# One table re-layout on another DMA queue, small loads later, denser table building in a two-block transformer

## The chip, the core and the metric

The kernel runs on one core of a Trainium2 chip. The metric is the device time of one execution in microseconds (us): the median of three runs of the kernel before is 1490.93 us (1490.72 to 1493.30). About 0.2 % of it, 3 us, is what a measurement of this kernel can tell from no change.

## What is computed

One sequence of 256 tokens of width 1024 passes through two transformer blocks of two layers each, all in float32. The first block has a pooling and recurrent mixer, a banded attention, a cross attention to a memory and two MLPs. The change touches the end of the first block and most of the second:

```python
def second_block(x, ...):
    h = x
    for i in range(DEPTH):                       # DEPTH = 2
        u = rms_norm(h, norm_mix[i])
        if i % 2 == 0:
            mix = diff_attention(u, attn_w_qkv, q_gain, k_gain, lam_vecs, subln_gain, w_o, lam, cos, sin)
        else:
            mix = s5_layer(u, a_re, a_im, log_dt, b_re, b_im, c_re, c_im, d_skip, w_glu)
        h = h + mix
        h = h + square(relu(rms_norm(h, norm_ffn[i]) @ w_up)) @ w_down      # 1024 -> 4096 -> 1024
```

`diff_attention` makes q, k and v with one 1024x3072 weight, normalises and rotates q and k (cos, sin, two gains), and subtracts lam times a second softmax from the first. `s5_layer` is a two-way complex state-space scan over 64 groups of 16 channels, then `gelu`, then a 1024x2048 gated product (`w_glu`). The scan is computed in blocks of eight tokens: from the parameters alone the kernel first builds tables (called e, g, and t) that turn the scan inside a block into matrix products.

## The kernel before

Every large product is done on TensorE (PE) as three single-pass products of split operands, hi x hi, lo x hi and hi x lo. So each weight tile takes three steps ahead of its products: a DMA on the queue of SyncE (SP) into a `raw` tile (L42), a rounding copy `whi` on ScalarE (ACT, L47 or, with a gain, L53), and the rest `wlo` on VectorE (DVE, L49 or L58). There are four `raw` buffers and ten `whi`/`wlo` pairs. A DMA into `raw` is issued when the `wlo` that last read that buffer is done.

A scheduler decides the order of the instructions of each engine when the kernel is built; on the chip each engine then runs its list in that order and waits at the head of it. The same holds for SP's list of DMA issues and for those of GpSimd (POOL). Each DMA of SP has one of eight completion semaphores in turn, and an issue also waits for the DMA that had this semaphore before.

The tables of the scan don't depend on the tokens, so they are built beside two MLPs: `ssm_tables` is a generator, and `mlp` advances it by `rate` per step (`step`, 49 of them in an MLP; what is left runs at `step(1000)` near its end). Blocks 0 to 7 are built in the last MLP of the first block (632 to 847 us of the span) and blocks 8 to 15 in the first MLP of the second block (980 to 1183 us, called ffb0). Each block writes e (`d_e`), g (`d_g`) and a kernel of lags (`d_kl`) to device memory. At the end of each half two DMAs re-layout `d_kl` into `d_ks`, and eight DMAs `d_ks` into `d_tt`, the table t (L1450 to L1456), all of them issued by POOL.

Between the two MLPs comes the differential attention (`diff`, 847 to 980 us). Its weights follow those of the MLP on SP. `rotations` combines cos, sin and the gains (L661 to L674); `part` makes the products with the weights, k first; `prep` normalises and rotates, and its `turned` transposes the result `z` on PE (tile `tq`, L742). In front of `part` stand the residual `X` (L187 to L200) of the last MLP, for token tiles t0 and t1, and its transposes `tp` (L140) into `hh` and `hl`.

After ffb0 comes the scan stage (`ssm`, 1183 to 1288 us). It copies X into `xp` (L1522), transposes it (`utp`), and for each quarter b: products with e (`zt`, L1561), transposes `z`, a rotation on DVE (`ra`, `zb`), the scan (`so`, L1589), a reversal on ACT (`sr`), two products with phases on DVE (`h0`, `h1`, L1610 and L1611), the products with t and g (`yp`), and gelu; then `ytp`, and the products `val` and `gp` with `w_glu`. `ssm_prefetch` loads some tables ahead, and `ssm` puts two tables of g and two of e (e4, e5) into `raw` buffers, behind the first four tiles of `w_glu` that use the same four buffers.

Of the kernel before, what the change touches and what calls it, by code (L numbers as in the profile page):

```python
# [413 lines left out]
class Attn:  # L414
# [224 lines left out]
    def diff(self, pool, w_qkv, gain, q_gain, k_gain, lam_vecs, subln, w_o, cos2, sin2, done):  # L639

        nc = self.nc
        cs = pool.tile([128, 2, 64], F32, tag="cos", name="cos")
        sn = pool.tile([128, 2, 64], F32, tag="sin", name="sin")
        nc.sync.dma_start(out=cs, in_=cos2.rearrange("(t p) e -> p t e", p=128))
        nc.sync.dma_start(out=sn, in_=sin2.rearrange("(t p) e -> p t e", p=128))
        gq, gk = (pool.tile([128, 64], F32, tag="g" + nm, name="qkg") for nm in "qk")
        nc.sync.dma_start(out=gq, in_=q_gain.partition_broadcast(128))
        nc.sync.dma_start(out=gk, in_=k_gain.partition_broadcast(128))
        sg = pool.tile([128, KT], F32, tag="sg", name="sg")
        nc.sync.dma_start(out=sg, in_=subln)  # L650
        lv = pool.tile([128, 4, 64], F32, tag="lv", name="lv")
        nc.sync.dma_start(out=lv, in_=lam_vecs.partition_broadcast(128))
        nlam = pool.tile([128, 1], F32, tag="nlam", name="nlam")
        tabs = {}

        def rotations():
            for nm, g in (("k", gk), ("q", gq)):
                ta = pool.tile([128, 2, 64], F32, tag="ta" + nm, name="ta")
# [485 lines left out]
class Ssm:  # L1144
# [225 lines left out]
    def ssm_tables(self, blocks, bc4, gain, d_rows, dmask):  # L1370
# [6 lines left out]
        with self.tc.tile_pool(name="tab", bufs=1, reuse_waits="tile") as pool:  # L1377
# [73 lines left out]
            nc.gpsimd.dma_start(out=ks[a0:a1, :, :, 0:112], in_=kl5[a0:a1, :, 1, :, 32:144])  # L1451
            yield
            n = 4 * (a1 - a0)
            for r in range(8):
                src = bass.AP(self.d_ks.tensor, self.d_ks.offset + 4 * a0 * 16 * 240 + r * 16, [[240, 16], [3840, n], [1, 128]])
                nc.gpsimd.dma_start(out=self.d_tt[r * 16:r * 16 + 16, 4 * a0:4 * a1, :], in_=src)  # L1456
            yield

    def ssm_prefetch(self):

        self.pre_pool = self.tc.tile_pool(name="pre", bufs=1, side="right", reuse_waits="tile")
        self.pre = pool = self.pre_pool.__enter__()
        self.tbs = {}
        self.unit = {}
        self.rho = pool.tile([128, NG], F32, name="rho")
        self.nc.sync.dma_start(out=self.rho, in_=self.d_rho)
        for b in range(2):
            self.load_phases(b)
        for q in range(4):
            t = pool.tile([128, 1024], F32, name=f"e{q}")  # L1470
            self.load_units(t, "e", q)
        for q in range(2):
            self.load_units(pool.tile([128, 1024], F32, tag=f"w{q}", name=f"t{q}"), "t", q)
# [17 lines left out]
    def load_phases(self, b):  # L1491

        t = self.pre.tile([128, 3, 16, 32], F32, tag="tbs", name="tbs", bufs=2)
        self.nc.sync.dma_start(out=t, in_=self.d_c[b].rearrange("p (a g c) -> p a g c", a=3, g=16))
        self.tbs[b] = t
# [241 lines left out]
def first_block(c, A):  # L1737
    tc, nc = c.tc, c.nc
    for l in range(2):
# [38 lines left out]
        with tc.tile_pool(name=f"ff{l}", bufs=1, reuse_waits="tile") as pool:  # L1778
            if l == 1:
                c.later.append(lambda: reorder(c))  # L1780
            c.mlp(pool, A["w_ff1"][l], gc[2], A["w_ff2"][l], lambda t, a, q: c.residual(t, a, post, q), perm=l == 1,
                  fill=tables(c, A, range(8)) if l == 1 else c.ssm_scalars(A["ssm_a_re_2"], A["ssm_a_im_2"], A["ssm_log_dt_2"], c.sgn),
                  rate=0.7 if l == 1 else 0.2)

# [14 lines left out]
def tables(c, A, blocks, last=False):  # L1799
    yield from c.ssm_tables(blocks, A["ssm_bc"], A["ssm_g"], c.d_rows, c.dmask)  # L1800
    if last:
        c.ssm_prefetch()


def second_block(c, A, out):
# [5 lines left out]
    with tc.tile_pool(name="ffb0", bufs=1, reuse_waits="tile") as pool:  # L1811
        c.mlp(pool, A["ffn_w_up_2"][0], c.gcols[:, 8, :], A["ffn_w_down_2"][0], lambda t, a, q: c.residual(t, a, None, q, feat=False),
              fill=tables(c, A, range(8, 16), last=True), rate=0.85)
    with tc.tile_pool(name="ssm", bufs=1, reuse_waits="tile") as pool:
# [84 lines left out]
```

## Time and profile before

| what | value |
|---|---|
| median of the runs | 1490.93 us |
| the profiled execution | 1488.93 us |
| its span | 1487.2 us |
| PE busy | 1414.7 us, 95 % |
| DVE busy | 1103.8 us, 74 % |
| ACT busy | 859.4 us, 58 % |
| POOL busy | 234.4 us, 16 % |
| mean granted TensorE clock | 0.985 |

The span is the time from the first to the last instruction in the profiled execution; that execution took 1.73 us more than its span, and 2.0 us less than the median. PE's share is that of an engine that has its next product ready nearly always, so a change shows in PE's gaps: they add up to 72.5 us. A row of the waits names the instruction that waited, what it waited for, the microseconds in total, how often, and the longest. Stage limits are read from the timeline; all times of the trace count from the start of the span.

### The profile page before, as it was taken

To read this page: it belongs to the slowest core of one execution; us is meant where nothing else is said; L and a number is where in the kernel's file an instruction comes from. 1 tells how busy PE (TensorE), PEld (TensorE's weight loads), DVE (VectorE), ACT (ScalarE), POOL (GpSimd) and SP (SyncE) were. 2 spreads that over 40 slices of the span, in tenths; PEclk is the share of its full clock that TensorE was granted. 3 is DMA by queue.
4 is the path that set the end of the run, shared out by engine and by line. 5 is a ranking of instruction groups with operands and counts; after the bars stand their busy time and mean duration, and the time that the engine had idled before them with its cause. 6 is when DMAs were issued, how large, how long until landed. Compare 5 with 4: busy or idle time off the path is not lost.

```text
span 1487.2 us, 25549 instructions
## 1 busy us (share of the span) xinstructions
PE 1414.7 (95%) x9668; PEld 1231.5 (83%) x9668; DVE 1103.8 (74%) x1965; ACT 859.4 (58%) x1480; POOL 234.4 (16%) x290
## 2 busy tenths in 40 slices
PE   8899999999999999999999789999999878999997
PEld 8897888998889798878888667888889666889895
DVE  7996658997676866569998589889995487665651
ACT  7475547565564665566656557667656463554540
POOL 1232001000010000014634210033551200000000
PEclk9999999999999999999999999999999998999999
DMA  8465535475875356366677734357779977455640
GB/s 302 143 198 170 185 125 177 157 257 193 287 256 184 119 180 200 112 207 207 220 242 265 254 124 142 100 161 241 238 236 334 346 280 262 153 187 180 210 159 29
DMA packets 121236, 298.26 MB, mean 201 GB/s; under 512 B 15129, under 2 KB 24121, under 8 KB 120473
## 3 DMA queue, kind: packets, MB, share of 16 engines
q1 hardware_dynamic: 113848, 271.40, 55.3%
q0 software_dynamic: 7264, 25.24, 4.6%
q8 instruction: 76, 1.25, 0.3%
q14 instruction: 48, 0.39, 0.1%
HBM read 270.15 MB, written 31.62 MB: 203 GB/s over the span
## 4 chain that ended last, share of the span: by engine, by line
PE 73%; DVE 13%; DMA 6%; issue 4%; ACT 3%; POOL 1%; SPq 0%; DVEq 0%; ACTq 0%; POOLq 0%
PE ffacc L217 7%; PE ffacc L219 7%; PE ffacc L218 7%; PE ffps L224 5%; PE ffps L226 5%; PE ffps L225 5%; PE pacc L219 4%; PE pacc L218 4%; PE pacc L217 4%; DVE wlo L58 3%; PE pb L225 3%; PE pb L224 3%; PE pb L226 3%; DMA raw<-in_w_ff 2%; PE ffps L219 2%
## 5 line engine op out<-in xcount | busy, mean ns | idle before, releaser
L58 DVE SCALAR_TENSOR_TENSOR wlo<-raw,gcols,whi 128x512 fp32r<-128x512 f32 (+1 forms) x456 | 356.7, 826 | 75.6 <-ACT whi L53 75.3
L53 ACT ACTIVATE whi<-raw,gcols 128x512 fp32r<-128x512 f32 (+1 forms) x456 | 317.0, 745 | 104.4 <-PE pb L226 17.3
L47 ACT ACTIVATE whi<-raw 128x1024 fp32r<-128x1024 f32 x176 | 182.8, 1055 | 155.6 <-DMA raw<-in_w_ff 59.3
L49 DVE TENSOR_TENSOR wlo<-raw,whi 128x1024 fp32r<-128x1024 f32 x172 | 210.1, 1241 | 84.1 <-ACT whi L47 80.1
L224 PE MATMUL ffps<-hh,whi 128*128 128x256 f32 x768 | 220.2, 287 | 2.7 <-ACT eo L1419 1.5
L226 PE MATMUL ffps<-hl,whi 128*128 128x256 f32 x768 | 218.2, 284 | 0.0
L225 PE MATMUL ffps<-hh,wlo 128*128 128x256 f32 x768 | 217.6, 283 | 0.0
L217 PE MATMUL ffacc<-whi,ah 128*128 128x512 f32 x512 | 204.7, 400 | 0.0
L219 PE MATMUL ffacc<-whi,al 128*128 128x512 f32 x512 | 202.2, 395 | 0.0
L218 PE MATMUL ffacc<-wlo,ah 128*128 128x512 f32 x512 | 202.1, 395 | 0.0
L224 PEld LDWEIGHTS ffps<-hh,whi 128*128 128x128 f32 x768 | 146.0, 190 | 5.3 <-ACT eo L1419 2.0
L225 PEld LDWEIGHTS ffps<-hh,wlo 128*128 128x128 f32 x768 | 145.7, 190 | 0.6
L226 PEld LDWEIGHTS ffps<-hl,whi 128*128 128x128 f32 x768 | 145.8, 190 | 0.0
L219 PEld LDWEIGHTS ffacc<-whi,al 128*128 128x128 f32 x512 | 96.4, 188 | 22.7
L217 PEld LDWEIGHTS ffacc<-whi,ah 128*128 128x128 f32 x512 | 96.5, 188 | 22.5 <-issue 1.8
L218 PEld LDWEIGHTS ffacc<-wlo,ah 128*128 128x128 f32 x512 | 96.5, 189 | 20.8
L225 PE MATMUL pb<-hh,wlo 128*128 128x256 f32 x352 | 101.2, 289 | 2.6 <-DVE wlo L58 2.6
L224 PE MATMUL pb<-hh,whi 128*128 128x256 f32 x352 | 101.2, 290 | 2.2 <-ACT whi L53 2.2
L226 PE MATMUL pb<-hl,whi 128*128 128x256 f32 x352 | 100.8, 287 | 0.0
L171 POOL TENSOR_TENSOR r<-r,mhalf 128x1 f32<-128x1 f32 x32 | 23.3, 730 | 463.9 <-DVE r L170 457.4
L303 ACT ACTIVATE relu<-ffps 128x512 f32<-128x512 f32 x64 | 43.8, 685 | 54.9 <-PE ffps L226 36.4
L225 PEld LDWEIGHTS pb<-hh,wlo 128*128 128x128 f32 x352 | 68.4, 195 | 3.4 <-DVE wlo L58 3.3
(488 smaller groups left out, 3024.9 us busy)
## 6 DMA issues: line engine op xcount, KB each, us to landing
raw<-in_w_ff SPq DMA_DIRECT2D x128, 512.0 KB, 4.6
raw<-in_ffn_w_up SPq DMA_DIRECT2D x64, 512.0 KB, 4.7
raw<-in_ffn_w_down SPq DMA_DIRECT2D x64, 512.0 KB, 4.6
raw<-in_w_mem_kv SPq DMA_DIRECT2D x32, 512.0 KB, 4.7
raw<-in_w_qkv SPq DMA_DIRECT2D x24, 512.0 KB, 4.7
raw<-in_attn_w_qkv SPq DMA_DIRECT2D x24, 512.0 KB, 5.0
raw<-in_w_in_ab SPq DMA_DIRECT2D x20, 512.0 KB, 6.5
raw<-in_w_mem_q SPq DMA_DIRECT2D x16, 512.0 KB, 4.6
```

The lines of the kernel that those rows point to most:

```text
L47: nc.scalar.activation(out=hi, in_=src, func=AF.Copy)
L49: eng.tensor_tensor(out=lo, in0=src, in1=hi.bitcast(F32), op=ALU.subtract)
L53: nc.scalar.activation(out=hi[:, a], in_=src[:, a], func=AF.Copy, scale=g)
L58: nc.vector.scalar_tensor_tensor(out=lo[:, a], in0=src[:, a], scalar=g, in1=hi[:, a].bitcast(F32), op0=ALU.mult, op1=ALU.subtract)
L171: nc.gpsimd.tensor_tensor(out=r, in0=r, in1=self.mhalf[:, 0:1], op=ALU.pow)
L217: nc.tensor.matmul(o, xh, wh[:, s], start=first, stop=False)
L218: nc.tensor.matmul(o, xh, wl[:, s], start=False, stop=False)
L219: nc.tensor.matmul(o, xl, wh[:, s], start=False, stop=last)
L224: nc.tensor.matmul(out, wh, xh, start=first, stop=False)
L225: nc.tensor.matmul(out, wl, xh, start=False, stop=False)
L226: nc.tensor.matmul(out, wh, xl, start=False, stop=last)
L303: nc.scalar.activation(out=o, in_=ps if view is None else ps.rearrange("p (f c j) -> p f c j", f=2, j=8), func=AF.Relu)
```

## The change

1. In `diff` the six loads of cos, sin, the two gains, the sub-layer gain and the lambda vectors move into `rotations`, which is called after the first half of the first products.
2. The eight DMAs that write `d_tt` go from POOL's queue to SP's. The generator pauses three times instead of once between `d_ks` and them.
3. `ssm_prefetch` becomes a generator that pauses before its loads of t.
4. `load_phases` for the quarters b = 2 and 3 goes from SP's queue to POOL's.
5. The rate at which the tables are built goes from 0.7 to 0.9 and, in ffb0, from 0.85 to 0.95.

```diff
@@ diff
-        nc.sync.dma_start(out=cs, in_=cos2.rearrange("(t p) e -> p t e", p=128))
-        nc.sync.dma_start(out=sn, in_=sin2.rearrange("(t p) e -> p t e", p=128))
...
-        nc.sync.dma_start(out=lv, in_=lam_vecs.partition_broadcast(128))
...
         def rotations():
+            nc.sync.dma_start(out=cs, in_=cos2.rearrange("(t p) e -> p t e", p=128))
+            nc.sync.dma_start(out=sn, in_=sin2.rearrange("(t p) e -> p t e", p=128))
...
+            nc.sync.dma_start(out=lv, in_=lam_vecs.partition_broadcast(128))
@@ ssm_tables
-            yield
+            for _ in range(3):
+                yield
             n = 4 * (a1 - a0)
             for r in range(8):
...
-                nc.gpsimd.dma_start(out=self.d_tt[r * 16:r * 16 + 16, 4 * a0:4 * a1, :], in_=src)
+                nc.sync.dma_start(out=self.d_tt[r * 16:r * 16 + 16, 4 * a0:4 * a1, :], in_=src)
@@ ssm_prefetch
+        yield
         for q in range(2):
             self.load_units(pool.tile([128, 1024], F32, tag=f"w{q}", name=f"t{q}"), "t", q)
@@ load_phases
-        self.nc.sync.dma_start(out=t, in_=self.d_c[b].rearrange("p (a g c) -> p a g c", a=3, g=16))
+        q = self.nc.gpsimd if b > 1 else self.nc.sync
+        q.dma_start(out=t, in_=self.d_c[b].rearrange("p (a g c) -> p a g c", a=3, g=16))
@@ the MLP of layer 1, tables 0 to 7
-                  rate=0.7 if l == 1 else 0.2)
+                  rate=0.9 if l == 1 else 0.2)
@@ tables
-        c.ssm_prefetch()
+        yield from c.ssm_prefetch()
@@ ffb0, tables 8 to 15
-              fill=tables(c, A, range(8, 16), last=True), rate=0.85)
+              fill=tables(c, A, range(8, 16), last=True), rate=0.95)
```

The change moves instructions in the lists of the engines. Three places are shown; a number behind a name is that of the buffer's tile, and lines below the edits count one to three more than before.

The list of DVE where the MLP of layer 1 ends and the attention begins: `y`, `r` and `X` are the residual of token tile t0, `wlo` are the attention's weights, `qkg` to `nlam` are `rotations`. Before:

```order
L187 TENSOR_TENSOR y_9234<-ffacc0_7393,gB_6955 128x512
L170 TENSOR_SCALAR r_9243<-ms_9240 128x1
...
L58 SCALAR_TENSOR_TENSOR wlo_9655<-raw_9652,gcols_109,whi_9654 128x512 x2
L58 SCALAR_TENSOR_TENSOR wlo_9663<-raw_9660,gcols_109,whi_9662 128x512 x2
L661 TENSOR_SCALAR qkg_9348<-qkg_9348 128x64
...
L674 TENSOR_SCALAR nlam_9356<-nlam_9356 128x1
L194 TENSOR_TENSOR r_9243<-r_9243,rsq_8337 128x1
L200 SCALAR_TENSOR_TENSOR X_90<-y_9234,r_9243,X_90 128x512 x2
```

The same list of the changed kernel:

```order
L187 TENSOR_TENSOR y_9234<-ffacc0_7412,gB_6955 128x512
L170 TENSOR_SCALAR r_9243<-ms_9240 128x1
L194 TENSOR_TENSOR r_9243<-r_9243,rsq_8443 128x1
L200 SCALAR_TENSOR_TENSOR X_90<-y_9234,r_9243,X_90 128x512 x2
L58 SCALAR_TENSOR_TENSOR wlo_9396<-raw_9393,gcols_109,whi_9395 128x512 x2
...
L674 TENSOR_SCALAR nlam_9350<-nlam_9350 128x1
L58 SCALAR_TENSOR_TENSOR wlo_9557<-raw_9554,gcols_109,whi_9556 128x512
```

The residual of t0 stands ahead of the weights and of `rotations` now; the seventh weight of the attention (`wlo_9557`) stands behind `rotations`, where eight weights stood in front of it before.

The list of SP at the same place in the changed kernel; `raw_9534` is the sixth weight of the attention and `raw_9554` the seventh:

```order
L42 DMA raw_9534<-in_attn_w_qkv_2 128x2x512
L1457 DMA d_tt_102<-d_ks_101 16x32x128 x7
L651 DMA cos_9344<-in_cos 128x2x64
L652 DMA sin_9345<-in_sin 128x2x64
L653 DMA qkg_9346<-in_attn_q_gain_2 128x64
L654 DMA qkg_9347<-in_attn_k_gain_2 128x64
L655 DMA sg_9348<-in_attn_subln_2 128x8
L656 DMA lv_9349<-in_attn_lambda_2 128x256
L42 DMA raw_9554<-in_attn_w_qkv_2 128x2x512
```

Before, eleven weights of the attention stood ahead of cos, and no `d_tt`; now six do.

The list of DVE from the end of ffb0 into the scan stage: `wlo_13092` to `wlo_13110` are the first four tiles of `w_glu`, `so` the scan of the first quarter, `ra_13272` the start of the second. Before:

```order
L49 TENSOR_TENSOR wlo_13104<-raw_13101,whi_13103 128x1024
L49 TENSOR_TENSOR wlo_13110<-raw_13107,whi_13109 128x1024
...
L1522 TENSOR_SCALAR xp_13035<-X_90,r_12965 32x16x16 x11
L1522 TENSOR_SCALAR xp_13035<-X_90,r_13022 32x8x16 x22
...
L1589 SCALAR_TENSOR_TENSOR so_13031<-rt_13029,zb_13030 128x528 x2
L1577 TENSOR_TENSOR ra_13272<-z_13195,tbs_12716 128x512
```

The same list of the changed kernel:

```order
L1525 TENSOR_SCALAR xp_13035<-X_90,r_13022 32x8x16 x22
...
L1592 SCALAR_TENSOR_TENSOR so_13031<-rt_13029,zb_13030 128x528 x2
L1613 TENSOR_TENSOR h0_13296<-sr_13265,tbs_12621 128x1024
L1614 TENSOR_TENSOR h1_13297<-sr_13265,tbs_12621 128x1024
L49 TENSOR_TENSOR wlo_13092<-raw_13089,whi_13091 128x1024
L49 TENSOR_TENSOR wlo_13098<-raw_13095,whi_13097 128x1024
L49 TENSOR_TENSOR wlo_13104<-raw_13101,whi_13103 128x1024
L49 TENSOR_TENSOR wlo_13110<-raw_13107,whi_13109 128x1024
L1580 TENSOR_TENSOR ra_13272<-z_13195,tbs_12623 128x512
```

The four `wlo` of `w_glu` stood ahead of the scan stage and stand behind its first `h1` now, and the copies `xp` of t0 (11 of them) have moved ahead of those of t1 and of the residual of t1.

## Rows read from the trace of the kernel before

**Rows 1.** The page: busy time, share of the span and instructions of each engine.

```profile
PE 1414.7 (95%) x9668; PEld 1231.5 (83%) x9668; DVE 1103.8 (74%) x1965; ACT 859.4 (58%) x1480; POOL 234.4 (16%) x290
```

**Rows 2.** The waits of PE over the whole span.

```profile
PE tp L140 <- issue: 11.1, 1, 11.1
PE utp L1538 <- DVE xp L1522: 9.2, 1, 9.2
...
PE tq L742 <- DVE z L736: 2.0, 1, 2.0
```

**Rows 3.** Stretches: length, busy time by engine (instructions), clock, DMA share, GB/s.

```profile
847.00:859.00 12.00, 0.91 (x5) 0.67 (x4) 9.51 (x30) 5.30 (x11) 0.00 (x0) 0.71 0.77 250
859.00:870.00 11.00, 11.00 (x49) 8.84 (x48) 6.23 (x14) 7.46 (x19) 1.65 (x3) 0.85 0.03 10
```

**Rows 4.** Timeline of PE at the attention's start: start, us, instruction, idle before.

```profile
858.36 1.94 PE L140 MATMUL tp<-ident,X 128*128 128x128 f32 x8 [11.09 <-issue]
```

**Rows 5.** Timeline of DVE at the attention's start.

```profile
853.23 0.20 DVE L661 TENSOR_SCALAR qkg<-qkg 128x64 f32<-128x64 f32 x1 [0.87 <-DMA qkg<-in_attn_q_gain]
...
856.17 0.29 DVE L669 TENSOR_TENSOR lp<-lv 128x128 f32<-128x128 f32 x1 [1.18 <-DMA lv<-in_attn_lambda]
...
857.51 1.41 DVE L200 SCALAR_TENSOR_TENSOR X<-y,r,X 128x512 f32<-128x512 f32 x2
...
874.75 2.91 DVE L733 TENSOR_TENSOR z<-kc,tb 128x512 f32<-128x512 f32 x1
877.59 1.21 DVE L713 TENSOR_REDUCE ss<-junk 128x16 f32<-128x1024 f32 x1
...
886.25 1.29 DVE L736 TENSOR_TENSOR z<-z,r 128x512 f32<-128x512 f32 x2
```

**Rows 6.** Timeline of POOL at the end of the first table set.

```profile
834.22 5.09 POOL L1456 DMA_DIRECT2D d_tt<-d_ks  x8 [2.19 <-DMA d_ks<-d_kl]
839.38 0.77 POOL L171 TENSOR_TENSOR r<-r,mhalf 128x1 f32<-128x1 f32 x1
```

**Rows 7.** Stretches in the two MLPs that build tables, columns as in rows 3.

```profile
750.00:800.00 50.00, 48.95 (x395) 43.22 (x394) 47.21 (x73) 32.40 (x56) 23.75 (x27) 1.00 0.73 245
...
1050.00:1100.00 50.00, 50.00 (x409) 44.53 (x408) 48.43 (x75) 27.61 (x52) 27.94 (x30) 1.00 0.71 240
```

**Rows 8.** Timeline of DVE, end of ffb0 and copies of X.

```profile
1175.68 2.36 DVE L49 TENSOR_TENSOR wlo<-raw,whi 128x1024 fp32r<-128x1024 f32 x2 [0.74 <-ACT whi L47]
...
1185.31 10.59 DVE L1522 TENSOR_SCALAR xp<-X,r 32x256 f32<-32x256 f32 x33
```

**Rows 9.** Timeline of DVE in the scan stage, second quarter.

```profile
1205.29 0.67 DVE L1577 TENSOR_TENSOR ra<-z,tbs 128x512 f32<-128x512 f32 x1
...
1207.78 1.22 DVE L1610 TENSOR_TENSOR h<-sr,tbs 128x1024 f32<-128x1024 f32 x1
...
1211.18 2.41 DVE L1589 TENSOR_TENSOR_SCAN so<-rt,zb 128x528 f32<-128x528 f32 x2
```

**Rows 10.** Timeline of ACT there: the last reversal of the first quarter.

```profile
1206.24 0.63 ACT L1593 ACTIVATE sr<-so 64x512 f32<-64x512 f32 x1
```

**Rows 11.** Timeline of SP: the two tables of e into raw buffers.

```profile
1176.94 1.45 SPq L1482 DMA_DIRECT2D raw<-d_e  x2
```

**Rows 12.** DMA issues of the page: count, KB each, median us to landing.

```profile
raw<-in_ffn_w_down SPq DMA_DIRECT2D x64, 512.0 KB, 4.6
...
e<-d_e SPq DMA_DIRECT2D x14, 512.0 KB, 7.0
...
d_ks<-d_kl POOLq DMA_DIRECT2D x2, 256.0 KB, 4.7
```

**Rows 13.** Timeline of PE in the scan stage.

```profile
1198.99 0.43 PE L1561 MATMUL zt<-raw,ut 128*32 128x128 f32 x8
...
1248.65 3.05 PE L1617 MATMUL yp<-g,h 128*32 128x128 f32 x104
...
1260.90 0.50 PE L217 MATMUL val<-whi,hh 128*128 128x512 f32 x1 [1.16 <-ACT hh L1643]
```

More of the change, by code (lines that the diff above doesn't have):

```diff
@@ L643, in diff @@
         sn = pool.tile([128, 2, 64], F32, tag="sin", name="sin")
-        nc.sync.dma_start(out=cs, in_=cos2.rearrange("(t p) e -> p t e", p=128))
-        nc.sync.dma_start(out=sn, in_=sin2.rearrange("(t p) e -> p t e", p=128))
         gq, gk = (pool.tile([128, 64], F32, tag="g" + nm, name="qkg") for nm in "qk")
-        nc.sync.dma_start(out=gq, in_=q_gain.partition_broadcast(128))
-        nc.sync.dma_start(out=gk, in_=k_gain.partition_broadcast(128))
         sg = pool.tile([128, KT], F32, tag="sg", name="sg")
-        nc.sync.dma_start(out=sg, in_=subln)
         lv = pool.tile([128, 4, 64], F32, tag="lv", name="lv")
-        nc.sync.dma_start(out=lv, in_=lam_vecs.partition_broadcast(128))
         nlam = pool.tile([128, 1], F32, tag="nlam", name="nlam")
@@ L656, in rotations @@
         def rotations():
+            nc.sync.dma_start(out=cs, in_=cos2.rearrange("(t p) e -> p t e", p=128))
+            nc.sync.dma_start(out=sn, in_=sin2.rearrange("(t p) e -> p t e", p=128))
+            nc.sync.dma_start(out=gq, in_=q_gain.partition_broadcast(128))
+            nc.sync.dma_start(out=gk, in_=k_gain.partition_broadcast(128))
+            nc.sync.dma_start(out=sg, in_=subln)
+            nc.sync.dma_start(out=lv, in_=lam_vecs.partition_broadcast(128))
             for nm, g in (("k", gk), ("q", gq)):
```

## The prediction

> **What bounds the kernel now.** I read the page's busy times first: PE works 1414.7 us [rows 1], so its gaps hold 72.5 us of the span of 1487.2, and only what opens, closes or shifts a gap can move the time. Next I read the waits of PE [rows 2]. The longest is the one ahead of the transposes `tp` at the start of the attention, 11.1 us; the second is that of `utp` for `xp` at the start of the scan stage, 9.2 us. The table by stretches shows what the first one costs beyond itself: from 847 to 859 the granted clock was 0.71, and from 859 to 870, with PE busy all the time, 0.85 [rows 3], where 1.00 is the level of 2.4 GHz. The timelines of PE, DVE, SP and POOL at these two places, and the lists of instructions of both kernels, then tell what the change moves.
>
> **The start of the attention: a gain.** PE ends the MLP at 858.36 - 11.09 = 847.27 [rows 4]; call this T. What it waits for is X of t0, which DVE begins at 857.51 [rows 5]. X depends on nothing but the MLP's own result and `r` of POOL, 839.38 to 840.15 [rows 6]; it is late because it stands behind sixteen `wlo` and behind `rotations` in DVE's list, and these wait for weights, for a gain (0.87 us) and for lv (1.18 us) [rows 5]. In the changed list X of t0 stands right behind its `r`, and `tp` of t0 stands in the middle of the MLP's last products. `r` is early too: POOL spent 834.22 to 839.31 on the eight issues of `d_tt` ahead of it [rows 6]. So the gap of 11.1 us goes, and with it the slow clock; of the 11.0 us at clock 0.85 the loss was 0.15 x 11.0 = 1.65 us [rows 3].
>
> What is late next? Before, PE reached the first `tq` when the first half of `z` was rotated, at 886.25 + 0.65 = 886.9 [rows 5], T + 39.6. Of this PE idled 11.1 and 2.0 [rows 2] and lost 1.65 to the clock, so its own work is 24.9, and without any wait the gain would be 14.7. But the seventh weight `wlo_9557` now stands behind `rotations` and `z` on DVE. The 48 products of k take 48 x 0.22 (11.0 us over 49 instructions, [rows 3]) = 10.6, the second `tp` 1.0 and its wait about 0.4, so k is done at T + 12. Four ACT passes at 0.63 [rows 10] make it T + 14.5; `ss` 1.21, thirteen small steps at 0.2, `rotations` about 2.5 without its waits, then z at 0.7 + 2.9 + 1.2 [rows 5] make it T + 25.6. PE has products for the six weights it holds until about T + 18.4, and stands some 7 us. The 6.6 us of products that are left then end near T + 32, a gain of 7.6. Without the new stand the gain is 14.7, and with the raw tile of that weight late as well (it is issued behind seven `d_tt` and six small loads) 4. I take 8, near the working.
>
> A rule that bears on the gap: the Trainium skill (TensorE: Matmul & The Clock Gate, Why this matters for your kernels) says that gaps in the matmul stream throw the clock back to its lower level. The trace agrees, with 0.71 and 0.85 behind the gap of 11.1 us. By that rule the new stand of 7 us would be paid again in clock; then the gain is about 1 us smaller, which the ends above hold.
>
> **The scan stage: a loss.** Two shifts work against each other. First, of the 33 copies `xp`, 10.59 us [rows 8] or 0.32 each, the 11 of t0 now run before X of t1 is there, which is 3.5 us less on DVE; with ACT's and POOL's copies beside them I take 2.5 of the 9.2.
>
> Second, the four `wlo` of `w_glu` ran before the scan stage; the last two of them ended at 1178.04 [rows 8]. So SP could load e4 and e5 into their `raw` buffers at 1176.94 [rows 11], and PE had them at 1198.99 [rows 13]. In the changed list these four `wlo` stand behind `h1` of the first quarter. The last `sr` of that quarter ended at 1206.87 [rows 10]; 2.5 earlier is 1204.4. Two `h` at 1.15 make it 1206.7, four `wlo` at 1.18 [rows 8] 1211.4. Only then can SP issue e5, and behind it in SP's list the rest of the tables: e6 to e11, t and g. A load of 512 KB took 4.6 us in the median where DMA had room and those of e 7.0 [rows 12]: e5 lands at 1216, e7 between 1217 and 1219. PE's `zt` of the second quarter moves from 1198.99 to about 1217, `ra` from 1205.29 [rows 9] to about 1219. From `ra` to the scan there were 5.9 us with 2.3 of `h` between [rows 9], which now run earlier, so the scan comes at 1219 + 3.6 = 1222.6, or 1223.5 with the later landing, in place of 1211.18: 12 us late. Nothing in the later quarters takes less DVE time than before, so this is carried to the last quarter. There part of it can vanish: the last `yp` were done between `val` products, until 1251.7 [rows 13], and `val` of the second half began at 1260.90; PE had `val` of the first half to do meanwhile. I take 3 off for this. The net, with the 2.5 in it, is +9. The low end is +3, where most of the delay falls into time that PE fills with `val`; the high end is +14, where the g of the last quarter and the tiles 5 to 8 of `w_glu`, issued behind them, take 7.0 in place of 4.6.
>
> **The denser tables.** In the MLP of layer 1 DVE was busy 47.21 of 50 us beside 48.95 of PE, in ffb0 48.43 beside 50.00 [rows 7]. The rates grow by 0.9/0.7 = 29 % and 0.95/0.85 = 12 %. If a third of DVE's time there is table work, 16 us in 50 (an estimate), that is 4.6 and 1.9 us more per 50, where 2.8 and 1.6 are free. Over some 150 us DVE falls back by 5 us in the first and by 1 in the second. Ten pairs of `whi` and `wlo` at 12 products of 0.22 are 26 us of cover for PE, so most of that is hidden. I take +2 (-2 to +6) and +1 (0 to +5, since PE had no gap there to lose).
>
> **`d_tt` on SP.** Eight issues leave POOL, 5.09 us there [rows 6], and come to SP, whose list then waits for `d_ks`, 4.7 us from issue to landing [rows 12]. The weights behind it are late by at most as much, which the 26 us of cover hide: 0 (-1 to +5; the top where the cover is used up by the denser tables). The Trainium skill (DMA: Bandwidth & Descriptors, Issuing engines are not separate DMA queues) says that all issuing engines feed the same DMA engines, so another issuer only saves issue time. The rows agree as far as they go: what POOL loses is the 5.09 us in front of `r`. By that rule the move by itself speeds up no transfer, and the sum holds nothing for it. The pauses and `load_phases` on POOL, which has nothing else to do in the scan stage, count 0.
>
> **The sum.** -8 + 9 + 2 + 1 + 0 = +4 on the profiled execution of 1488.93 us: 1492.9. That execution lies 2.0 below the median of the runs, so on the median it is 1490.93 + 4, about 1495 us.
>
> **Rivals.**
> - *The stage hides the late tables.* Against my reading, PE or the order of the quarters absorbs the 12 us; then the scan stage ends within 2 us of before or 2 earlier, and the gain of the attention is left: 1490.9 - 8 + 0 to 3 = 1483 to 1486, faster. For it: PE is busy 95 % and has `val` to put into gaps; against it: the list of DVE, which can't pass the four `wlo`.
> - *The two cancel.* Scan stage +5, tables +1: -2, 1488 to 1494, no change that can be told.
> - *The seventh weight takes the gain back.* If `wlo_9557` and the weights behind it hold PE for 11 us or more, the attention gains 4 or less; with +12 from the scan stage and +3 from the tables it is 1500 to 1506. It decides where the weight comes later than T + 30. For it: DMA moved only 10 GB/s from 859 to 870 [rows 3], so weights were held by full buffers before too.
> - *SP stands in front of `d_ks`.* By 4.7 us or more, with no cover: +5 on all of the above. It needs the ring to be empty when the denser tables end, and rows 7 show PE with no gap then.
>
> **How the numbers follow.** Forecast 0.46 (about half the way to each neighbour: 1493 to 1500), hidden 0.27, cancel 0.15, taken back with SP's stand 0.12. One measurement tells 0.2 %, 3 us, from no change. Slower by more: 0.46 less 0.06 that falls under the bound, plus 0.12, that is 0.52; faster: 0.27 plus 0.02 of the cancelling case, 0.29; the same: the rest, 0.13 and 0.06, 0.19. The range reaches from the hidden case with a full gain, 1482, to the middle of the taken-back case, 1505.
>
> **What would show it.** Right: `tp` of t0 lies before the end of the MLP's last products with no wait over 1 us, the clock stays at 1.00 behind T, and PE waits some 7 us in the attention's first products for `wlo` L58; in the scan stage `zt` reads `raw` near 1217 less whatever came earlier, with a wait of 15 us or more for e, and `val` of the second half is about 9 us later against the end of ffb0. Wrong: a scan stage as long as before from `utp` to `val`, a wait of PE for `wlo` of over 10 us in one of the two MLPs, or weights that wait on SP behind `d_tt`.

## The result, and the profile after

The changed kernel takes 1531.1 us in the median (1529.34 to 1532.7, four runs) against 1490.83 us of the kernel before on the same chip (1487.41 to 1493.3, four runs): a ratio of 1.0266, 95 % interval 1.0251 to 1.0281. It is 40 us slower, where +4 was forecast and 1505 was the top of the range. The direction was right; the size was not.

The page of the changed kernel, the same row as [rows 1]; its span is 1528.2 us:

```profile
PE 1431.6 (94%) x9668; PEld 1242.3 (81%) x9668; DVE 1103.1 (72%) x1965; ACT 858.5 (56%) x1480; POOL 221.6 (15%) x276
```

PE's gaps grew from 72.5 to 96.6 us, 24 more. But PE is also busy 17 us longer with the same 9668 products, at a lower clock (mean granted clock 0.970, before 0.985). So the loss can't be read from the gaps alone.

I cut both spans at the same events in the timeline of PE: the first product `ffps` of the MLP of layer 1, its last `ffacc`, the first `tq`, the attention's last `pacc`, the last `ffacc` of ffb0, the first `utp`, the last `ytp`.

| stage | before | after | difference | in the prediction |
|---|---|---|---|---|
| MLP of layer 1, tables 0 to 7 | 209.2 | 226.0 | +16.8 | +2 (-2 to +6) |
| to the first `tq` | 39.8 | 32.5 | -7.3 | -8 |
| rest of the attention | 99.1 | 106.6 | +7.5 | not in the sum |
| ffb0, tables 8 to 15 | 197.4 | 201.0 | +3.6 | +1 (0 to +5) |
| to `utp` | 9.2 | 6.2 | -3.0 | -2.5 |
| `utp` to the last `ytp` | 65.8 | 88.7 | +22.9 | +11.5 |
| all else | | | +0.5 | 0 |
| sum | | | +41.0 | +4 |

The same stages by busy time, cut at the same events; length, busy time by engine (instructions), clock, DMA share, GB/s. The order is MLP of layer 1, rest of the attention, ffb0, and from there to the last `ytp`; the row to the first `tq` is left out. The kernel before:

```profile
638.10:847.27 209.17, 200.28 (x1401) 173.30 (x1399) 168.90 (x255) 127.67 (x216) 80.07 (x90) 0.99 0.71 235
...
887.09:986.20 99.11, 96.27 (x535) 78.78 (x536) 86.93 (x199) 67.19 (x143) 8.72 (x10) 1.00 0.41 129
986.20:1183.60 197.40, 197.40 (x1401) 171.76 (x1399) 159.61 (x239) 112.87 (x198) 77.97 (x88) 1.00 0.76 265
1183.60:1258.60 75.00, 53.96 (x1010) 42.66 (x1010) 60.09 (x91) 41.41 (x68) 4.00 (x9) 0.86 0.77 280
```

The changed kernel:

```profile
638.80:864.80 226.00, 206.23 (x1410) 178.82 (x1409) 170.41 (x261) 129.19 (x220) 75.91 (x83) 0.96 0.64 213
...
897.30:1003.80 106.50, 100.69 (x538) 81.42 (x537) 93.18 (x211) 75.68 (x158) 8.65 (x10) 0.97 0.48 150
1003.80:1204.80 201.00, 197.78 (x1401) 171.71 (x1399) 159.79 (x246) 111.26 (x199) 69.42 (x83) 1.00 0.71 247
1204.80:1299.80 95.00, 59.14 (x1010) 46.02 (x1010) 59.05 (x81) 40.01 (x65) 4.85 (x9) 0.79 0.64 236
```

In the MLP of layer 1 PE's gaps went from 8.9 us (209.17 - 200.28) to 19.8, and its busy time rose by 5.9, of which 1.0 is `tp` of t0, moved in here. In ffb0, where PE had no gap, it has 3.2 us. From there to the last `ytp` the gaps went from 21.0 to 35.9, and the busy time rose by 5.2 at a clock of 0.79.

The longest waits of PE over the whole span of the changed kernel, to be read beside [rows 2] (what waited, what for, us in total, how often, the longest):

```profile
PE zt L1564 <- DMA raw<-d_e: 19.8, 2, 19.6
PE ffps L224 <- ACT eo L1419: 7.3, 2, 4.8
PE utp L1541 <- DVE xp L1525: 6.2, 1, 6.2
```

The 11.1 us of `tp` are gone and a wait of 19.6 us for a table of e has come.

**The scan stage.** Timelines of PE, DVE and SP of the changed kernel, to be read beside [rows 8, 9, 11, 13]:

```profile
1211.03 1.94 PE L1541 MATMUL utp<-ident,xp 128*128 128x128 f32 x8 [6.19 <-DVE xp L1525]
1237.16 0.65 PE L1564 MATMUL zt<-raw,ut 128*32 128x128 f32 x8 [19.57 <-DMA raw<-d_e]
```

```profile
1226.44 1.22 DVE L1614 TENSOR_TENSOR h<-sr,tbs 128x1024 f32<-128x1024 f32 x1
1227.57 4.63 DVE L49 TENSOR_TENSOR wlo<-raw,whi 128x1024 fp32r<-128x1024 f32 x4
1244.66 0.69 DVE L1580 TENSOR_TENSOR ra<-z,tbs 128x512 f32<-128x512 f32 x1 [12.46 <-PE z L1573]
...
1248.57 2.41 DVE L1592 TENSOR_TENSOR_SCAN so<-rt,zb 128x528 f32<-128x528 f32 x2
```

```profile
1231.09 1.46 SPq L1484 DMA_DIRECT2D raw<-d_e  x2
1232.60 3.63 SPq L1484 DMA_DIRECT2D e<-d_e  x6
```

This is the chain that was forecast: the four `wlo` of `w_glu` run behind the first `h1`, the `raw` buffers come free from 1228.7 on (1227.57 and a quarter of 4.63), SP issues e4 and e5 behind that, at 1231.09, and six more e behind them, and PE stands at `zt`. From `utp` to `zt` it is 26.1 us; the prediction's own numbers give 1217 - (1192.8 - 2.5) = 26.7. Stretches of the wait and of what follows it show why it cost more than the wait:

```profile
1217.00:1231.00 14.00, 0.59 (x6) 0.35 (x4) 11.94 (x13) 7.77 (x11) 0.66 (x1) 0.69 0.11 31
1237.00:1250.00 13.00, 12.04 (x226) 9.45 (x230) 5.27 (x7) 2.36 (x5) 0.00 (x0) 0.64 1.03 413
```

In the first stretch DMA moves 31 GB/s: nothing lacks bandwidth, SP waits for buffers. In the second all tables that stood behind e4 come at once, DMA is full at 413 GB/s, and PE's clock is 0.64: eight `zt` products take 0.65 us where they took 0.43 [rows 13]. So from `zt` to `ra` it is 7.5 us; the prediction allowed 2. The scan of the second quarter comes 37.5 us behind `utp`, 18.4 before.

**The start of the attention.** PE and ACT of the changed kernel, beside [rows 4, 5]:

```profile
858.18 1.04 PE L140 MATMUL tp<-ident,X 128*128 128x128 f32 x8
...
888.00 1.22 PE L217 MATMUL acc<-whi,hh 128*128 128x512 f32 x2 [5.59 <-ACT whi L53]
```

```profile
887.13 0.20 ACT L672 ACTIVATE ls<-ls 128x2 f32<-128x2 f32 x1 [8.85 <-DVE ls L671]
887.24 3.16 ACT L53 ACTIVATE whi<-raw,gcols 128x512 fp32r<-128x512 f32 x5
```

`tp` of t0 has no wait, and the new stand is there with 5.6 us. It comes through ACT's list: the `whi` of the seventh weight stands behind the exponential `ls` of `rotations`, which waits for DVE. The prediction had put it on DVE's `wlo`.

**The rest of the attention.** The last stretch of the attention in the kernel before, and then in the changed one:

```profile
959.89:986.20 26.31, 26.06 (x143) 22.11 (x142) 19.27 (x35) 17.80 (x32) 3.31 (x7) 1.00 0.50 153
```

```profile
970.10:1003.80 33.70, 30.05 (x152) 24.25 (x151) 24.06 (x48) 22.54 (x48) 3.69 (x7) 0.90 0.48 153
```

Each row begins 72.8 us behind the first `tq`. What is left from there takes 7.4 us longer, 26.3 against 33.7, with 152 products against 143; these nine more are the least of it: the clock falls to 0.90, and PE has gaps of 3.7 us where it had 0.3. In the changed list 24 of the 96 score products `dsc` stand behind the last product with a weight of q, k or v, where six stood before, so few products are left there to fill the waits of the softmax. The traces of all the kernels below agree: in the seven that have 24 there, it is 39.5 to 42.4 us from the last product with such a weight to the last `pacc`, and in the seven that have six it is 30.2 each time.

### The profile page after: what moved, and what is told of

Its sections match the earlier page's. It is cut to its first block, busy times and chain, and to the rows that moved or that the text cites. A ratio compares the mean times of both kernels' runs of the same rounds, so it can differ in the third digit from the quotient of the medians.

```text
span 1528.2 us, 25503 instructions
## 1 busy us (share of the span) xinstructions
PE 1431.6 (94%) x9668; PEld 1242.3 (81%) x9668; DVE 1103.1 (72%) x1965; ACT 858.5 (56%) x1480; POOL 221.6 (15%) x276
## 5 line engine op out<-in xcount | busy, mean ns | idle before, releaser
L219 PEld LDWEIGHTS ffacc<-whi,al 128*128 128x128 f32 x512 | 96.3, 188 | 22.9
L218 PEld LDWEIGHTS ffacc<-wlo,ah 128*128 128x128 f32 x512 | 96.4, 188 | 20.9
L224 PE MATMUL pb<-hh,whi 128*128 128x256 f32 x352 | 100.6, 288 | 1.3 <-ACT whi L53 1.3
```

The costliest lines, as they stand in the source:

```text
L218: nc.tensor.matmul(o, xh, wl[:, s], start=False, stop=False)
L219: nc.tensor.matmul(o, xl, wh[:, s], start=False, stop=last)
L224: nc.tensor.matmul(out, wh, xh, start=first, stop=False)
```

## The experiments

Theory A, formed on these two traces: the loss is made of three losses that add up, the denser tables in the MLP of layer 1, the move of `d_tt` to SP in the attention, and, where `d_tt` on SP meets the rate of 0.95, the wait at the scan. Each time is the median of the runs, each ratio is against the kernel before on the same chip, and the times of stages are those of one profiled execution.

**e1: the small loads alone.** The six loads of `diff` go into `rotations`, all else as before.

> The kernel before with the six small loads moved into rotations and nothing else. Its lists of DVE, PE and SP at the start of the attention read as those of before (eleven weights ahead of cos, X of t0 behind rotations). Theory A (the loads move nothing, the gain at the attention's start comes from the d_tt issues that left POOL): 1490.8 within 2 us, and the gap ahead of tp still 11 us. Rival B (the prediction's wording, where the moved loads free X): 1483, with no gap ahead of tp.

1488.95 us, ratio 0.9989 (0.9976 to 1.0001). PE waits 11.6 us at `tp` as before, and no stage moved by over 0.7 us. This part does nothing: in the trace the engines' lists, SP's among them, keep their order. The early `tp` of the changed kernel therefore isn't its doing.

**e2: the two rates alone.**

```diff
-                  rate=0.7 if l == 1 else 0.2)
+                  rate=0.9 if l == 1 else 0.2)
...
-              fill=tables(c, A, range(8, 16), last=True), rate=0.85)
+              fill=tables(c, A, range(8, 16), last=True), rate=0.95)
```

> The kernel before with the rates 0.9 and 0.95 and nothing else. Theory A (the denser tables cost the MLP of layer 1 its 17 us, by short waits of PE for table steps, and ffb0 its 4): 1508 to 1513, the last product of the layer-1 MLP near 864, the gap ahead of tp, the rest of the attention and the scan stage as before. Rival B (the MLP loses through SP, which waits with d_tt in front of the weights): 1490 to 1494, the MLP's end near 847.

1509.6 us, ratio 1.0125 (1.0107 to 1.0144), as A says. The MLP of layer 1 takes 224.3 us, 15.1 more than before, and ffb0 200.7, 3.3 more. The scan stage, which A had as before, takes 69.6, 3.8 more. Which waits carry the loss of the MLP, read from the changed kernel (PE, 640 to 848 us; the end of the stage adds none):

```profile
PE ffps L224 <- ACT eo L1419: 7.3, 2, 4.8
PE klag L1426 <- issue: 3.4, 3, 2.1
PE fftp L345 <- ACT relu L307: 3.1, 1, 3.1
PE klag L1426 <- POOL cmt L1166: 1.9, 1, 1.9
PE ffps L224 <- ACT kl L1432: 1.5, 1, 1.5
PE etp L1418 <- ACT eo L1419: 1.5, 1, 1.5
```

But for `fftp`, which waits as long before, all of them are waits at a table's product (`etp`, `klag`) or for the copy of one (`eo`, `kl`). Together they are 15.6 us, and 14.3 in e2 itself; in the kernel before the same kinds came to 5.3. No row names a `wlo`. The table products stand in PE's list among the MLP's, and PE waits at the head for their inputs.

**e3: `d_tt` on SP alone**, with its three pauses.

```diff
-            yield
+            for _ in range(3):
+                yield
...
-                nc.gpsimd.dma_start(out=self.d_tt[r * 16:r * 16 + 16, 4 * a0:4 * a1, :], in_=src)
+                nc.sync.dma_start(out=self.d_tt[r * 16:r * 16 + 16, 4 * a0:4 * a1, :], in_=src)
```

> The kernel before with the eight d_tt issues on SP and the three pauses, and nothing else. Theory A: the MLP of layer 1 ends near 847 as before, the second half of the attention loses 7 us (24 of the score products stand behind its last weight products in PE's list, 6 before), three of the four w_glu tiles are converted between xp and the first scan, so the tables e4 and e5 come late by part of what the changed kernel shows: 5 to 12 us in the scan stage. In all 1497 to 1508. Rival B (SP's waits cost the MLP 17 us): the MLP ends near 864 and the time is 1512 or more.

1518.66 us, ratio 1.0187 (1.0161 to 1.0213). The MLP of layer 1 is as before (209.9), so its loss belongs to the rates. But this part alone costs 28 us, more than A said: the attention behind the first `tq` takes 117.5 us (+18.4), and from `utp` to the last `ytp` it is 80.9 (+15.1, with 10.8 us of waits of `z` for ACT's `zc`), less 4.1 to the first `tq` and 3.0 at `utp`. Nor do the parts add up as A has it: e2 and e3 cost 19 and 28 us, 47 together, where the changed kernel loses 40. SP in this kernel:

```profile
845.10 10.57 SPq L42 DMA_DIRECT2D raw<-in_attn_w_qkv  x7
855.76 6.36 SPq L1457 DMA_DIRECT2D d_tt<-d_ks  x7
870.15 64.04 SPq L42 DMA_DIRECT2D raw<-in_attn_w_qkv  x10
```

The first 36.4 us behind the first `tq`, before and then in e3:

```profile
887.09:923.49 36.40, 34.38 (x183) 27.00 (x184) 35.71 (x89) 23.99 (x54) 2.40 (x1) 1.00 0.41 134
```

```profile
883.60:920.00 36.40, 31.31 (x148) 24.01 (x149) 25.96 (x70) 17.19 (x44) 2.38 (x1) 0.86 0.02 5
```

PE gets 148 products done instead of 183, with DMA at 5 GB/s. ACT's timeline in e3 tells why no weight comes:

```profile
873.86 0.71 ACT L53 ACTIVATE whi<-raw,gcols 128x512 fp32r<-128x512 f32 x1
...
905.66 0.56 ACT L780 ACTIVATE dp<-dsc,mx,r 128x256 f32<-128x256 f32 x1 [7.46 <-PE dsc L455]
...
910.01 1.35 ACT L53 ACTIVATE whi<-raw,gcols 128x512 fp32r<-128x512 f32 x2
```

From 874.6 to 910.0 ACT makes no `whi`: the next one stands behind the softmax's eight `dp`. So the `raw` buffers stay full, SP waits (ten issues take 64 us), and PE has no weight products to put beside the scores. Here too 24 score products stand behind the last weight product.

**e4: the changed kernel with `d_tt` on POOL again** (`nc.gpsimd` in that one line).

> The changed kernel with the eight d_tt issues back on POOL, all else as changed. Theory A (d_tt on SP makes the late w_glu tiles and the late tail of the attention, the rates make the slower MLPs): as the run with the rates alone, 1508 to 1513, with zt reading the raw tables without a wait of 19.6 us. Rival C (the moved loads of phases, the pause in the prefetch or the rates make the w_glu tiles late): the wait of zt stays and the time is 1525 or more.

1511.77 us, ratio 1.0129 (1.0108 to 1.0149), as A says: 19 us come back. The three pauses are kept here, so this is the queue alone. From `utp` to the last `ytp` it is 64.9 us with no wait over 1.2 us at `zt`, and the rest of the attention 100.6. The wait at `tp` is back as well (9.2 us; 8.6 in e2 and 8.3 in e3), so of the parts of the change the early `tp` needs two, `d_tt` on SP and the rate of 0.9. It isn't the time that POOL spent on the issues: in e2 POOL is through with them at 823.5, 29 us ahead of its `r` for t0, and in e3 it has none, and PE waits in both. In sum, from the MLP's end to its last `pacc` the attention takes 138.9 us before, 139.1 in the changed kernel and 139.2 here: `d_tt` on SP gains 7 us at the start and gives them back at the end.

**e5: the changed kernel with both old rates.**

> The changed kernel with the old rates 0.7 and 0.85. Theory A: both MLPs as before (209 and 197 us), the attention as in the run with d_tt on SP alone (35.7 to the first tq, then 117.5), and the scan stage shorter than there, because the phases of the quarters 2 and 3 no longer stand in SP's list ahead of the tables e8 and later: from zt on the raw tables to the last ytp some 63 us, where d_tt alone had 74. In all 1504 to 1511. Rival D (the phases on POOL change nothing): 74 stays and the time is 1517 to 1520.

1513.6 us, ratio 1.0152 (1.0127 to 1.0177). The MLP of layer 1 is back at 210.4 us and ffb0 at 197.4; the rest of the attention is 118.4, as in e3. The time lies between the ranges of A (1504 to 1511) and D (1517 to 1520). From the `zt` on the raw tables to the last `ytp` it is 66.1 us against 74.0 in e3, the one stage in which the two profiled executions differ by over 2 us (65.6 in e7 below). SP's lists of the two kernels differ first at `load_phases`, so these eight us are most likely the gain of the phases on POOL; between the medians it is 5, and the profiled execution of e5, 1508.07, is its fastest.

**e7: the changed kernel with the old rate in ffb0 alone** (0.85 for 0.95).

> The changed kernel with the old rate 0.85 in ffb0, 0.9 kept in the MLP of layer 1. In DVE's list one w_glu tile then stands ahead of the copies xp and three between xp and the first scan, none behind it. Theory A: the MLP of layer 1 keeps its 224 to 227 us, ffb0 goes back to 197, the wait ahead of zt on the raw tables is under 3 us: 1505 to 1512. Rival F (the scan stage's loss belongs to d_tt on SP alone, whatever the rate): the wait of about 19 us stays and the time is 1525 or more.

1511.57 us, ratio 1.0138 (1.0114 to 1.0161), as A says. One number takes the wait of 19.6 us away: `zt` of the second quarter comes 6.7 us behind `utp`.

```profile
1215.90 0.43 PE L1564 MATMUL zt<-raw,ut 128*32 128x128 f32 x8
```

In this list the four `wlo` of `w_glu` stand ahead of the scan. So neither SP nor the rate alone makes the wait; both together move those `wlo` behind `h1`.

**e6: the tables ahead of `w_glu`.** In the changed kernel the two g and two e tables take the `raw` buffers ahead of the first four tiles of `w_glu` (`seg_v.get(kt)`), not behind them. Rival E says that the tables are late for another reason, or that the later `w_glu` tiles take the gain back.

```diff
-        for kt in range(4):
-            seg_v.get(kt)
...
+        for kt in range(4):
+            seg_v.get(kt)
```

> The changed kernel with the two tables of g and the two of e loaded into the raw buffers ahead of the first four w_glu tiles, not behind them. Theory A (e4 and e5 are late because their raw buffers are held until the w_glu tiles are converted behind the first h1): the wait of 19.6 us ahead of zt on the raw tables goes, and the scan stage is 13 to 19 us shorter: 1512 to 1518. Rival E (the tables are late for another reason, or the w_glu tiles that come later now take it back in front of val): 1526 or more.

1527.97 us (1521.57 to 1533.92), ratio 1.0245 (1.0202 to 1.0289): the time of E, though its runs lie far apart and the profiled one is the slowest. e4 and e5 are in time now (`zt` 6.6 us behind `utp`), but e6 isn't. SP and then PE:

```profile
1222.84 12.05 SPq L42 DMA_DIRECT2D raw<-in_ssm_w_glu  x4
1234.94 3.73 SPq L1484 DMA_DIRECT2D e<-d_e  x6
```

```profile
1242.49 0.66 PE L1564 MATMUL zt<-e,ut 128*32 128x128 f32 x8 [19.28 <-DMA e<-d_e]
```

Now the tiles of `w_glu` wait for `raw` buffers at the head of SP's list, and six e tables, whose own buffers are free, stand behind them.

**e10: and the table loads on POOL's queue.** As e6, with the loads of e, t and g issued by GpSimd (but for those that `ssm_prefetch` issues).

```diff
-        self.nc.sync.dma_start(out=t, in_=src)
+        (q or self.nc.gpsimd).dma_start(out=t, in_=src)
```

> The changed kernel with the tables of g and e ahead of the w_glu tiles in the raw buffers, and all table loads of the scan stage issued by POOL, not by SP, so that they don't stand behind the w_glu tiles in one list. Theory A (the wait of 19 us is that of one list: whatever waits at its head for a raw buffer holds the tables behind it): no wait of zt over 5 us, from the first utp to the last ytp some 68 us in place of 88.8: 1508 to 1516. Rival E (the stage is bound by when the buffers come free, whoever issues): 1524 or more.

1530.84 us, ratio 1.0277 (1.0255 to 1.03): no gain, the time of E. POOL:

```profile
1230.18 0.63 POOL L1497 DMA_DIRECT2D tbs<-d_c  x1 [17.40 <-DVE h L1614]
1230.81 3.12 POOL L1484 DMA_DIRECT2D e<-d_e  x6
```

A load of phases that waits 17.4 us for `h1` to free its buffer heads POOL's list here, and the same six e stand behind it; PE waits 17.2 us at the same `zt`.

**e12: the phases back to SP.** As e10, with `load_phases` on SP for all quarters, so that nothing that waits heads POOL's list.

> The kernel after, with the g and e tables of the scan ahead of the gate's weight tiles in the list of the raw buffers, and these table loads issued by GpSimd; the three phases stay with the sync queue, so that no phase that waits stands ahead of the last e tiles in GpSimd's list. Theory A (the wait of 17 to 20 us at the scan is the wait at the head of an in-order list of issues, whichever engine has the list): no zt product waits over 10 us, first utp to last ytp 68 to 72 us instead of 88.7, the time 1510 to 1517. Rival E (the buffers come free late whoever issues, so the wait goes along): the wait of 17 us or more is at an e or a raw tile again, the time 1524 or more.

1525.69 us, ratio 1.0239 (1.0208 to 1.0269): A's time is missed, E's is met, and yet the wait is at neither an e nor a raw tile. All e are early at last (POOL issues six at 1209.66), and PE waits at `z`. PE, ACT and SP:

```profile
1240.10 1.11 PE L1572 MATMUL z<-ident,zc 128*128 128x128 f32 x4 [20.89 <-ACT zc L1564]
```

```profile
1236.72 1.06 ACT L47 ACTIVATE whi<-raw 128x1024 fp32r<-128x1024 f32 x1 [8.71 <-DMA raw<-in_ssm_w_glu]
1238.50 1.06 ACT L47 ACTIVATE whi<-raw 128x1024 fp32r<-128x1024 f32 x1 [0.73 <-DMA raw<-in_ssm_w_glu]
1239.47 0.58 ACT L1564 ACTIVATE zc<-zt 128x512 f32<-128x512 f32 x1
```

```profile
1226.39 0.33 SPq L1496 DMA_DIRECT2D tbs<-d_c  x1
1227.53 20.62 SPq L42 DMA_DIRECT2D raw<-in_ssm_w_glu  x6
```

The copy `zc` that PE needs has its input since 1218, and stands in ACT's list behind two `whi` of `w_glu`; their tiles stood on SP behind a phase that waited for `h`, and were then loaded with DMA full (411 GB/s from 1227 to 1237). So in e6 and e12 the tiles of `w_glu` stand ahead of what PE needs, on SP and then on ACT, and in e10 it is a load of phases that waits for `h1`. A and E both described one face of it. What these lists share is that the four tiles are in the middle of the scan; in e4 and e7, where they stand ahead of it, the long wait is absent. No run moved these tiles and nothing else, so that their place decides is argued, not shown.

**e8: lower rates**, 0.6 and 0.75, against rival G, that 0.7 is already at the flat bottom of the curve.

```diff
-                  rate=0.7 if l == 1 else 0.2)
+                  rate=0.6 if l == 1 else 0.2)
...
-              fill=tables(c, A, range(8, 16), last=True), rate=0.85)
+              fill=tables(c, A, range(8, 16), last=True), rate=0.75)
```

> The kernel before with the rates 0.6 and 0.75, the other way from the change. Theory A (table steps in PE's list wait for DVE, ACT and POOL, the more the denser they stand): the MLP of layer 1, 209 us at 0.7 and 224 at 0.9, comes to 203 to 208, ffb0 to 196 to 197: 1483 to 1490. Rival G (0.7 is at the bottom; what is left over runs in one lump near the MLP's end and costs there): 1493 or more.

1494.28 us, ratio 1.0021 (1.0009 to 1.0034): G. The MLP of layer 1 stays at 209.4 us, and ffb0 gets 5.1 longer. From 0.6 to 0.7 the stage is flat, at 0.9 it is 15 us longer.

**e11: the high rates with less work on DVE.** Rates 0.9 and 0.95 on the kernel before, and of table g's complex product four DVE operations less; POOL writes two plain products in its place, so g doesn't hold the complex product here.

```diff
-                    self.cmul(pool, gr[:, :, 0], gr[:, :, 1], pj(16), pj(24), vi(cr), vi(ci), neg_i=True, tag="cte", second=G)
+                    G.tensor_tensor(out=gr[:, :, 0], in0=pj(24), in1=vi(ci), op=MU)
+                    G.tensor_tensor(out=gr[:, :, 1], in0=pj(24), in1=vi(cr), op=MU)
```

> The kernel before with the rates 0.9 and 0.95, where the table g is wrong: the four DVE operations of its complex product are left out and POOL writes its two products straight into it, so POOL's work is unchanged and DVE has 22 us less in each of the two MLPs. Theory A1 (DVE, 96 % busy in the dense stretch, is what the table steps in PE's list wait for): the layer-1 MLP comes from 224 back to 208 to 214 us, ffb0 to 197: 1490 to 1497. Rival A2 (the order in ACT's and PE's lists, or POOL's share, is what waits): the MLP stays at 219 or more, 1503 or more.

1493.46 us, ratio 1.0018 (1.0004 to 1.0032), where e2 with the same rates takes 1509.6. The MLP of layer 1, e2 and then e11:

```profile
637.50:861.80 224.30, 205.59 (x1401) 177.54 (x1399) 170.18 (x258) 129.91 (x219) 79.75 (x90) 0.97 0.66 221
```

```profile
639.30:850.30 211.00, 199.91 (x1401) 173.64 (x1399) 152.31 (x225) 130.00 (x219) 73.77 (x90) 0.98 0.71 234
```

With 17.9 us less of DVE's time the stage is 13.3 us shorter, with ACT unchanged. PE then has a single long wait, 10.5 us at an `fftp`, and its table of waits names none at a table's product. So these waits hang on the work that was taken from DVE. Two things changed with it: POOL's same 90 instructions take 6.0 us less, and `klag`, which reads g, has a shorter chain in front of it; the run doesn't separate DVE's load from these. In ffb0 A1 is not met: with 14.7 us less of DVE's time (160.2 in e2) the stage takes 200.1 us, where A1 said 197 and e2 has 200.7.

```profile
987.00:1187.10 200.10, 197.85 (x1401) 171.71 (x1399) 145.47 (x207) 113.15 (x198) 70.27 (x88) 1.00 0.77 263
```

**e9: the gain without the price.** In the kernel before, `d_ks` and `d_tt` of the first half stay on POOL, but the program issues them in the first steps of the second half (two `d_ks` at block 8 of the tables, eight `d_tt` at blocks 10 to 13). The scheduler then spreads them over POOL's list: in the trace the `d_ks` go out at 832.9 and 840.5, and the `d_tt` between 854 and 900, through the attention and behind the `r` of t0.

```diff
+                if k == 8:
+                    self.turns[0]()
+                if k in (10, 11, 12, 13):
+                    for r in range(2):
+                        self.turns[1](2 * (k - 10) + r)
...
+            if a0 == 0:
+                self.turns = lags, turn
+                return
```

> The kernel before with the re-layouts of the first table set (its d_ks and its eight d_tt) issued by POOL from the second set's first steps in ffb0, not at the end of the layer-1 MLP. Rates, SP's queue and the small loads are as before. In the lists tp of t0 then stands in the middle of the MLP's last products, nine of the attention's weights stand ahead of rotations (ten before) and the score products stand as before. Theory A (X of t0 was late because POOL's list had the re-layouts ahead of r): the gap of 11.1 us goes, 37 us or less from the MLP's last product to the first tq in place of 39.8, the tail of the attention 99 us: 1478 to 1486. Rival H (what comes free is taken by the seventh weight, as in the changed kernel, or by the re-layouts in ffb0): 1488 to 1492.

1483.79 us, eleven runs, against 1491.12: ratio 0.9955 (0.994 to 0.9969). It beats both kernels. To the first `tq` it takes 32.9 us instead of 39.8; the MLP of layer 1, with `tp` of t0 inside it, takes 211.9, 2.7 more; and the rest stays as it was: 99.1 us for the rest of the attention, 197.4 for ffb0, 64.5 from `utp` to the last `ytp`. PE:

```profile
859.70 1.94 PE L140 MATMUL tp<-ident,X 128*128 128x128 f32 x8 [4.08 <-issue]
...
882.94 0.63 PE L742 MATMUL tq<-ident,z 128*128 128x128 f32 x4 [2.03 <-DVE z L736]
```

`tp` of t0 runs at 843.4 without a wait, and that of t1 waits 4.1 us (11.1 at t0 before, [rows 4]); only six score products stand behind the last weight product. So the gain at the attention's start is real and can be had by itself, without the move to SP and without the rates. Why the scheduler puts `tp` early here and in the changed kernel, but not in e1 to e5, no run shows.

## Why the prediction was wrong, step by step

- **The start of the attention, -8: right in size.** -7.3, with `tp` inside the MLP and a stand of 5.6 us, near the 7 forecast. The list that made the stand was ACT's, not DVE's, and the issues that left POOL, which the prediction named as what made `r` early, don't bring it alone (e3 waits 8.3).
- **The rest of the attention, no term: missed.** +7.5. I followed the lists to the first `tq` and counted what is behind it as unchanged. The score products that lost their cover stand in the same lists. e4 shows that `d_tt` on SP causes most of it (100.6 without), e3 and e5 that it can cost 18 us. In e3 the trace shows it, `whi` behind `dp` on ACT. In the changed kernel, where the loss is at the attention's end, that it is the 18 further products behind the last weight is argued from the list, from the stretch that lost the time and from the two groups of kernels (30.2 us with six, 39.5 and more with 24); no run moved them alone.
- **The denser tables, +2 in the MLP of layer 1: the term that failed most,** +16.8. The step that failed is "ten pairs of `whi` and `wlo` at 12 products of 0.22 are 26 us of cover for PE": I took the pairs as what stands between DVE's lag and PE. The waits are for the tables' own products, which stand in PE's list and have no such cover. I had seen DVE busy 47.21 and 48.43 of 50 us [rows 7] and called the remaining 3 us free; a lag of 5 us on DVE was what I worked out, and in e11 18 us less on DVE made the stage 13 shorter. The clock adds to it: of the 16.8 us, 10.9 are gaps and 5.9 are busy time (1.0 of it `tp`).
- **ffb0, +1: within its bounds,** +3.6. It is the rate's (e2: +3.3 without any other edit; e7 with the old rate: 197.0, -0.4). In the changed kernel PE's waits there are at tables' products too (1.7, 1.1 and 0.5 us), but less work on DVE doesn't take the loss away (e11: 200.1), so what makes it stays open.
- **`d_tt` on SP, 0: wrong.** I bounded the wait of SP for `d_ks` and the issue times, -1 to +5, and treated the move as one of issue. Its price is the place in the lists: 28 us alone (e3), 19 in the changed kernel (e4). The Trainium skill (DMA: Bandwidth & Descriptors, Issuing engines are not separate DMA queues) says that another issuer only saves issue time. For the transfers these runs agree: from issue to landing a `d_tt` takes 5.5 us in the median on POOL before, and on SP 5.9 in e3 and 4.5 in the changed kernel. But the new order of the engines' lists that comes with the move is worth more than the 5.09 us of issues [rows 6].
- **The scan stage: the mechanism was right to the list, the size was not.** `xp` gave 3.0 (2.5 forecast), and `zt` came 26.1 us behind `utp` (26.7). Then three things were off. From `zt` to `ra` it took 7.5 us and not 2, at a clock of 0.64 and with all tables on DMA at once, which is 5 more. The 3 us I took off for `val` were not to be had. And from the scan of the second quarter to the last `ytp` it took some 3 more instead of nothing. Together 11, from +11.5 to +22.9.
- **The loads, the pauses and the phases, 0.** Right for the loads (e1). The pauses were not tried alone. The phases on POOL were probably worth a gain of 5 to 8 (e3 against e5); whether the changed kernel has it, under its longer wait, no run shows. e10 shows that they can hold POOL's list as well.
- **The rivals.** "The stage hides the late tables" is refuted by the table of stages. "The seventh weight takes the gain back" did not happen where I put it (the stand is 5.6 us, not 11), though the gain was taken back, later. "The two cancel" is out with the time. "SP stands in front of `d_ks`" had the cost in the weights behind `d_tt`; in the MLP of layer 1 no wait of PE for a weight shows in e3 (209.9 us), and the cost came later, through the order. A rival in which the tables alone cost 15 us was absent; my own sign for "wrong", a long wait for `wlo`, would have missed it.

Left open: what holds ffb0, why the later quarters add 3 us, and whether the kernel e9 gains more with phases on POOL; neither was tried.

## What to carry to other kernels

Where an engine is some 95 % busy over a stretch, as DVE was here beside the MLP, don't take the rest as free for denser work, and count as cover only what stands in front of the very instructions that will wait: look for them in the list of the waiting engine. Where a scheduler makes the order, a DMA that moves to another queue can be an edit to the order of every engine: read the lists to the end of the next stage, not to the first place that gains. And when a wait moves along as one queue after another is relieved (19.6 us on SP, 17.2 on POOL, 20.9 through ACT), read in every list what stands in front of the instruction that waits, before relieving the first queue.

## What the runs showed that I had not expected

- The same 9668 products took 17 us more of PE's busy time (1414.7 to 1431.6), at a mean clock of 0.970 instead of 0.985; of a loss of 41 us in the span that is two fifths. In the 13 us behind the wait of 19.6 us at the scan the granted clock was 0.64, with PE busy 12.04 of them.
- Within 6 us DMA went from starved to full: 31 GB/s from 1217 to 1231, in the wait, and 413 GB/s from 1237 to 1250.
- One rate of 0.95 instead of 0.85 in ffb0 cost 19 us (e7 against the changed kernel). 4 of them are in ffb0 and the others in the scan stage behind it, where the four `wlo` of `w_glu` stand behind `h1` in one list and ahead of the scan in the other.
